# Dilated queries grouped by residue inside tiles of 128, and attention biases read as tables

## The chip, the cores and the metric

The kernel runs on one core of a Trainium2 chip. The metric is the device time of one execution in microseconds (us). The engines are TensorE (PE in the profile; its weight loads are listed apart as PEld), VectorE (DVE), ScalarE (ACT), GpSimd (POOL) and SyncE (SP), which issues most of the transfers (DMAs).

## The reference

One encoder layer and a final norm on 1024 tokens of width 1024, in float32.

```python
h = x
hn = rms_norm(h, norm_mix_g)
proj = hn @ w_in                              # q, k, v of 8 dilated and of 8 neighbourhood heads of 64
y_dil = dilated_mixture_attention(...)        # patterns (window, step): (128, 1), (512, 4), (2048, 16)
y_na  = neighbourhood_attention(..., rpb)     # 8 x 16 windows on a 16 x 64 grid, learned bias
h = h + concat(rms_norm(y_dil, g_out_dil), rms_norm(y_na, g_out_na)) @ w_out
h = h + hierarchical_moe(rms_norm(h, norm_ffn_g), ...)   # 1 of 4 groups, 2 of its 4 experts, width 256
y = rms_norm(h, norm_final_g)
```

The change lies in the dilated attention. A query at token t attends to the tokens t + j*d within half a window, for d = 1, 4 and 16; every score gets `- slope[head] * |distance|` with slope `0.5 ** (head + 1)`, and the three patterns are merged by their softmax denominators. Within the patterns of d = 4 and d = 16 a query meets only keys of its own residue modulo 4.

## The kernel before, in words

The kernel has three stages: norm, transposes and values (0 to about 120 us), attention (to about 530 us), and the router with 16 experts (to the end). Matrix products are in fp32r with each operand split in a high and a low part.

The attention stage works on eight pairs of heads, four dilated (`Dil`), then four of the neighbourhood kind (`Nbr`). Each pair has 16 steps, 8 for either head (`h` is 0 or 1, `n` is 0 to 7). The loop over steps (`for s in range(len(steps) + 4)`, L853) writes the order of all instructions by hand: step s issues the scores of its own step (`first`, with its matmuls on L411), the transposes of the probabilities of step s-2 (`second`, L509), and the product with the values of step s-3 (`third`, L534 and L545). Between these, `take` puts matmuls of the next pair's projection (L378), so that TensorE has work while the other engines do the softmax: `soft` on DVE (L424), the exponential on ACT (L430), and the evacuation in two parts (ACT L103, DVE L104).

In a dilated head the steps n = 0 to 3 are the near ones (d = 1 over a tile of 128 queries) and n = 4 to 7 the far ones, one for each residue r = n - 4 modulo 4. In each step two blocks of 128 queries are multiplied, each with the high and with the low part of the keys: four matmuls. The query block is the stationary operand (the weight load), the 256 keys are the moving one. Queries lie in `q_s` in the order of tokens, so a near block is 128 neighbouring columns and a far block is every fourth column:

```python
493                        qs = slice(512 * z + r, 512 * z + r + 509, 4)
```

Keys are already stored by residue. `fold` adds the two halves of a product and writes it to `ot`; in the far steps with r odd (L550) it writes two residues with a step of four columns. After the last step of a pair, `merge`, `merge2` and `store` weigh the near and the far result and store it to `y_dil` in DRAM (L558 to L601); these come in steps n = 1 to 3 of the next pair, which also hold the last projection matmuls of its queries and their evacuation (L401, L402). I call these steps the boundary of two pairs.

The bias of a dilated head is made on POOL in `prepare` (L462): a table of distances is halved in place for each head (L465) and the mask is added (L466). In a neighbourhood head POOL adds a mask that is loaded once to the learned bias (L623).

SP issues its DMAs strictly in the written order; a DMA that waits holds up all that are written behind it. Among them are the values (`va` L470 to L472, `vb` L477), the copy of keys into the other half of the partitions (`k_hh` L407), the projection weights (`w_raw` L152) and the stores.

Of the kernel before, what the change touches and what calls it, by code (L numbers as in the profile page):

```python
# [9 lines left out]
F32 = mybir.dt.float32  # L10
# [20 lines left out]
def shape_constants():  # L31

    p = np.arange(128)
    i, r = p // 4, p % 4
# [10 lines left out]
    mask = -8 * np.concatenate([m_a, m_b], 1).astype(np.float32)  # L45

# [12 lines left out]
    perm = np.zeros((128, 136), np.float32)  # L59
    perm[p, 4 * (p % 32) + 3] = 1.0  # L60
    perm[p, 132 + p // 32] = 1.0
# [7 lines left out]
    return {"dist": dist, "mask": mask, "na_mask": na_mask, "ident": np.eye(128, dtype=np.float32),  # L69
# [3 lines left out]
def build(nc, tc, a, ctx, dbg=None):  # L73
# [71 lines left out]
    with ExitStack() as att:  # L145
# [15 lines left out]
        factors = qk.tile([128, 2], F32, name="factors", bufs=1)  # L161
        perm = qk.tile([128, 136], F32, name="perm", bufs=1)
# [10 lines left out]
        with ExitStack() as ph:  # L173
# [125 lines left out]
            nc.vector.memset(factors[:, 0:1], 0.5)  # L299
            nc.vector.memset(factors[:, 1:2], 8.0)  # L300
# [37 lines left out]
        class Pair:  # L338
# [18 lines left out]
            def ps_view(self, ps, keys):  # L357
                if self.dil:
                    return ps.rearrange("p (i r) -> p r i", r=4) if keys else ps
                return ps.rearrange("p (r j c) -> p r j c", j=8, c=8)  # L360
# [48 lines left out]
            def scores(self, ps, h, qs, keys):  # L409
                for n, k in enumerate((self.kh, self.kl)):  # L410
                    nc.tensor.matmul(ps, self.q[h][:, qs], keys(k[h]), start=n == 0, stop=n == 1)  # L411
# [39 lines left out]
        class Dil(Pair):  # L451
# [22 lines left out]
            def late_loads(self, h):  # L474
                head = 2 * self.n + h
                vb = self.vb[h] = ap.tile([128, 8, 128], F32R, name="vb", tag="vb", bufs=1)
                nc.sync.dma_start(f(vb), vb_d[:, head * 128:(head + 1) * 128].rearrange("(k p) x -> p k x", p=128))  # L477

            def first(self, h, n):
# [4 lines left out]
                for z in range(2):  # L484
# [31 lines left out]
            def third(self, h, n, pt):  # L516
# [32 lines left out]
                if r % 2:  # L549
                    fold(self.ot[1][hs].rearrange("p (i r) -> p r i", r=4)[:, r - 1:r + 1], self.op,  # L550
                         lambda t: t.rearrange("p (r i) -> p r i", r=2))

            def merge(self):
# [3 lines left out]
                for h in range(2):  # L557
# [3 lines left out]
                                            perm[:, 132:136, None].to_broadcast([128, 4, 16]), op=ALU.mult)  # L561
                self.parts = parts

            def merge2(self):
                st, parts = self.stats, self.parts
                pb = bank("pt")
                for r in range(4):
                    nc.tensor.matmul(pb[:, 0:32], perm[:, 3 - r:131 - r], parts[:, :, :, 2 * r:2 * r + 2],
                                     start=r == 0, stop=r == 3)
                sb = ap.tile([128, 2, 2, 8], F32, name="sb")  # L570
                nc.vector.tensor_copy(sb.rearrange("p h z (q k) -> p k (h z) q", k=4),
                                      pb[:, 0:32].rearrange("p (k x q) -> p k x q", k=4, q=2))
                e = ap.tile([128, 2, 2, 8], F32, name="e")
                nm = ap.tile([128, 2, 8], F32, name="nm2")
# [4 lines left out]
                l2 = ap.tile([128, 2, 2, 8], F32, name="l2")  # L579
# [24 lines left out]
        class Nbr(Pair):  # L604


            def early_loads(self, h):
                if h == 0:
                    if self.n == 0:
                        Nbr.mask = ap.tile([128, 896], F32, name="na_mask", tag="mask", bufs=1)  # L610
                        nc.sync.dma_start(Nbr.mask, a["na_mask"])
                    self.nb = ap.tile([128, 2, 384], F32, name="nb", tag="dist", bufs=1)
                    nc.sync.dma_start(self.nb, nb_d[:, 2 * self.n:2 * self.n + 2, :])

            def prepare(self, h):
                head = 2 * self.n + h
                if h == 0:
                    nc.gpsimd.tensor_tensor(self.nb, self.nb, factors[:, 1:2, None].to_broadcast([128, 2, 384]),
                                            op=ALU.mult)
                bias = self.bias[h] = ap.tile([128, 896], F32, name="bias", tag="bias")  # L620
                nbv = self.nb[:, h].rearrange("p (r h c) -> p h r c", h=3, c=8)
                for c0, c1, h0, h1 in ((384, 640, 1, 3), (0, 384, 0, 3), (640, 896, 0, 2)):
                    nc.gpsimd.tensor_tensor(bias[:, c0:c1].rearrange("p (h r c) -> p h r c", r=16, c=8),  # L623
                                            Nbr.mask[:, c0:c1].rearrange("p (h r c) -> p h r c", r=16, c=8),
# [8 lines left out]
            def first(self, h, j):  # L633
# [6 lines left out]
                self.scores(sp[:, :n], h, slice(j * 128, j * 128 + 128), lambda k: k[:, c0 * 128:c1 * 128])  # L640
# [38 lines left out]
            def merge(self):  # L679
                self.rl = ap.tile([128, 8, 2], F32, name="rl")  # L680
# [172 lines left out]
        for s in range(len(steps) + 4):  # L853
# [14 lines left out]
            run_exps()  # L868
            run_slow(2)
# [925 lines left out]
```

## Time and profile before

| | us |
|---|---|
| median of 3 runs | 889.92 |
| lowest and highest run | 888.94, 892.41 |
| the profiled execution | 892.44 |
| its span in the trace | 890.7 |
| PE busy in the span | 832.3 (93%) |
| DVE, ACT, POOL busy | 558.5 (63%), 510.0 (57%), 220.9 (25%) |
| mean granted TensorE clock | 0.976 |

The span is the time from the first to the last instruction in the trace; the 1.7 us between it and the execution's time lie around it. A row of a timeline gives start, duration, engine, line, operation, output<-inputs, shape, count, and in brackets how long the engine had been idle and what ended that. Matmuls overlap, so the distance between two starts tells what one costs, and the duration does not. A `windows` row gives the busy time of each engine in a stretch, the granted clock, the mean busy share of the 16 DMA engines and the GB/s that they moved.

### The profile page before, as it was taken

The page shows a single profiled execution, that of the slowest core. Times are in us where ns is not written, and L with a number is a line of the kernel's source. Part 1 is how long each engine was busy: PE and PEld are TensorE (multiplying, and loading weights), DVE is VectorE, ACT ScalarE, POOL GpSimd, SP SyncE. Part 2 cuts the span into 40 slices and gives each one's busy share as a digit, 9 for nine tenths or more (in the row PEclk, how much of TensorE's full clock was granted, in tenths as well). Part 3 has the DMA queues.
Part 4 walks back from the last instruction along what each step waited for, and adds up shares of the span by engine and source line. Part 5 has one row for each costly group of instructions (what it writes and reads, how often), then busy time and mean ns, then how long its engine had stood idle before and what let it go on. Part 6 is the DMA issues. An engine that isn't in the chain of part 4 may idle for free. (4 is left out here: it accounts for less than half of the span.)

```text
span 890.7 us, 13312 instructions
## 1 busy us (share of the span) xinstructions
PE 832.3 (93%) x4492; PEld 693.2 (78%) x4492; DVE 558.5 (63%) x1249; ACT 510.0 (57%) x1079; POOL 220.9 (25%) x180
## 2 busy tenths in 40 slices
PE   8999999989999999999898999999799999999880
PEld 5888878979889888878787887887577787777760
DVE  4551125776767767666677753677786566959573
ACT  5441127757667576677575633543585566858570
POOL 4001122221232302332411100000442344635403
PEclk8999999999999999999999999998999999999995
DMA  6855452314343141534346747995798987999663
GB/s 238 286 210 165 126 159 65 105 48 108 96 136 105 54 137 48 148 100 120 76 160 195 265 144 239 357 343 216 233 354 250 317 220 209 357 324 304 181 257 121
DMA packets 129919, 168.72 MB, mean 189 GB/s; under 512 B 14875, under 2 KB 101403, under 8 KB 129824
## 3 DMA queue, kind: packets, MB, share of 16 engines
q1 hardware_dynamic: 119904, 143.58, 49.8%
q0 software_dynamic: 9936, 24.16, 9.8%
q8 instruction: 41, 0.67, 0.3%
q14 instruction: 38, 0.31, 0.1%
HBM read 129.93 MB, written 47.47 MB: 199 GB/s over the span
## 5 line engine op out<-in xcount | busy, mean ns | idle before, releaser
L103 ACT ACTIVATE pt_hi<-ps_pt 128x512 fp32r<-128x512 f32 (+2 forms) x128 | 67.6, 528 | 70.8 <-PE ps_pt L509 41.7
L378 PE MATMUL ps_mm<-xhi,w_lo 128*128 128x512 f32 x256 | 105.1, 411 | 1.1 <-POOL w_lo L104 1.1
L378 PE MATMUL ps_mm<-xlo,w_hi 128*128 128x512 f32 x256 | 105.0, 410 | 0.0
L378 PE MATMUL ps_mm<-xhi,w_hi 128*128 128x512 f32 x256 | 102.9, 402 | 0.0
L104 DVE TENSOR_TENSOR pt_lo<-ps_pt,pt_hi 128x512 fp32r<-128x512 f32 (+2 forms) x128 | 77.2, 603 | 31.8 <-ACT pt_hi L103 31.1
L104 POOL TENSOR_TENSOR w_lo<-w_raw,w_hi 128x1024 fp32r<-128x1024 f32 x16 | 38.3, 2392 | 229.5 <-ACT w_hi L103 229.5
L424 DVE CUSTOM_DVE_ANT_0 p<-ps_s,bias 128x256 f32<-128x256 f32 (+1 forms) x192 | 81.8, 450 | 18.2 <-PE ps_s L411 10.8
L104 DVE TENSOR_TENSOR g_lo<-raw_up,g_hi 128x1024 fp32r<-128x1024 f32 x64 | 75.5, 1220 | 25.2 <-ACT g_hi L103 25.1
L1419 PE MATMUL ps_mm<-g_hi,x_hi 128*128 128x512 f32 x184 | 76.0, 413 | 0.5 <-ACT x_hi L103 0.5
L1419 PE MATMUL ps_mm<-g_hi,x_lo 128*128 128x512 f32 x184 | 74.2, 403 | 2.2 <-DVE x_lo L104 2.2
L1419 PE MATMUL ps_mm<-g_lo,x_hi 128*128 128x512 f32 x184 | 73.9, 402 | 0.0
L430 ACT ACTIVATE p<-p,stats 128x256 f32<-128x256 f32 x128 | 63.7, 500 | 9.6 <-DVE stats L424 9.1
L103 ACT ACTIVATE g_hi<-raw_up 128x1024 fp32r<-128x1024 f32 x64 | 64.4, 1067 | 1.8 <-DMA raw_up<-in_w_up 0.8
L411 PE MATMUL ps_s<-k_hh,q_s 128*128 128x256 f32 (+1 forms) x192 | 60.7, 324 | 4.0 <-DMA k_hh<-k_hh 1.4
L411 PE MATMUL ps_s<-k_low,q_s 128*128 128x256 f32 (+1 forms) x192 | 62.6, 334 | 0.0
L411 PEld LDWEIGHTS ps_s<-k_hh,q_s 128*128 128x128 f32 x192 | 44.6, 232 | 10.9 <-DVE q_s L402 2.6
L378 PEld LDWEIGHTS ps_mm<-xhi,w_lo 128*128 128x128 f32 x256 | 48.7, 190 | 5.2 <-POOL w_lo L104 1.4
L1357 POOL DMA_INDIRECT xg<-hn_d,gi x30 | 41.3, 1377 | 40.1 <-PEq L1533 9.3
L378 PEld LDWEIGHTS ps_mm<-xhi,w_hi 128*128 128x128 f32 x256 | 48.7, 190 | 3.2
L378 PEld LDWEIGHTS ps_mm<-xlo,w_hi 128*128 128x128 f32 x256 | 48.4, 189 | 3.5
L411 PEld LDWEIGHTS ps_s<-k_low,q_s 128*128 128x128 f32 x192 | 44.6, 232 | 3.5
L430 ACT ACTIVATE p<-p,nm 128x384 f32<-128x384 f32 (+1 forms) x64 | 37.5, 586 | 15.2 <-DVE nm L424 14.8
(301 smaller groups left out, 2125.6 us busy)
## 6 DMA issues: line engine op xcount, KB each, us to landing
raw_up<-in_w_gate SPq DMA_DIRECT2D x32, 512.0 KB
raw_up<-in_w_up SPq DMA_DIRECT2D x32, 512.0 KB
raw_down<-in_w_down SPq DMA_DIRECT2D x16, 1024.0 KB
w_raw<-in_w_in SPq DMA_DIRECT2D x16, 512.0 KB
xt<-in_x SPq DMA_DIRECT2D x8, 512.0 KB
k_hh<-in_w_in SPq DMA_DIRECT2D x8, 512.0 KB
va_d<-vt SPq DMA_DIRECT2D x16, 256.0 KB
vb_d<-vt SPq DMA_DIRECT2D x8, 512.0 KB
```

Of the source, the lines that this page charges most:

```text
L103: nc.scalar.activation(hi, src, AF.Copy)
L104: (nc.gpsimd if pool else nc.vector).tensor_tensor(lo, src, f(hi), op=ALU.subtract)
L378: nc.tensor.matmul(ps, l[:, k, :], x[half][:, k, :], start=i == 0, stop=i == 23)
L411: nc.tensor.matmul(ps, self.q[h][:, qs], keys(k[h]), start=n == 0, stop=n == 1)
L424: nc.vector.tensor_tensor_reduce(out=p, in0=ps, in1=bias, scale=-0.125, scalar=3.0e38, op0=ALU.add, op1=ALU.min, accum_out=nm)
L430: nc.scalar.activation(p, p, AF.Exp, bias=nm, scale=-1.0, accum_out=l)
L1357: return nc.gpsimd.indirect_dma_start(out=x, out_offset=None, in_=src[:, :], in_offset=bass.IndirectOffsetOnAxis(ap=idx, axis=0), bounds_c ...
L1419: nc.tensor.matmul(ps, l[:, k, :], wt[:, k, :], start=i == 0, stop=i == 23)
```

## The change

1. The queries of a dilated pair are evacuated into `q_s` by residue inside each tile of 128: column 32r + i of a tile holds token 4i + r. The tables of distances and the merge's permutation follow that order; `ot` and `y_dil` hold it too, and `yd_load` puts tokens back in order when it reads `y_dil`.
2. A new step `regroup` copies a head's queries from `q_s` to a single buffer `qr`, where all 256 queries of a residue lie together. Four DMAs a head do so (eight half ones for the first head of a pair), each of 128-byte pieces. Far steps read `qr`.
3. The biases of the eight dilated heads come as finished tables from DRAM, one load a head. L465 and L466 go.
4. In a neighbourhood head the mask is loaded into the bias's buffer, once a head, and POOL adds the learned bias in place. Some small tiles of the merge have one buffer in place of two.

```diff
     p = np.arange(128)
-    i, r = p // 4, p % 4
+    i, r = p % 32, p // 32
...
+    bias = np.stack([np.float32(0.5 ** (h + 1)) * dist + mask for h in range(8)])
...
             def q_view(self, t, half):
                 if self.dil:
-                    return t[:, 512 * half:512 * half + 512]
+                    return t.rearrange("p (t r i) -> p t r i", r=4, i=32)[:, 4 * half:4 * half + 4]
...
             def early_loads(self, h):
-                if self.n == 0 and h == 0:
-                    Dil.dist = ap.tile([128, 768], F32, name="dist", tag="dist", bufs=1)
-                    Dil.mask = ap.tile([128, 896], F32, name="mask", tag="mask", bufs=1)[:, :768]
-                    nc.sync.dma_start(Dil.dist, a["dist"])
-                    nc.sync.dma_start(Dil.mask, a["mask"])
+                bias = self.bias[h] = ap.tile([128, 896], F32, name="bias", tag="bias")
+                nc.sync.dma_start(bias[:, :768], a["bias"][2 * self.n + h])
...
-                bias = self.bias[h] = ap.tile([128, 896], F32, name="bias", tag="bias")
-                nc.gpsimd.tensor_tensor(Dil.dist, Dil.dist, factors[:, 0:1].to_broadcast([128, 768]), op=ALU.mult)
-                nc.gpsimd.tensor_tensor(bias[:, :768], Dil.dist, Dil.mask, op=ALU.add)
...
+            def regroup(self, h, t0, t1):
+
+                if t0 == 0:
+                    self.qr = ap.tile([128, 1024], F32R, name="qr", bufs=1)
+                for r in range(4):
+                    nc.sync.dma_start(f(self.qr).rearrange("p (r t i) -> p r t i", r=4, i=32)[:, r, t0:t1],
+                                      f(self.q[h]).rearrange("p (t r i) -> p r t i", r=4, i=32)[:, r, t0:t1])
...
-                        qs = slice(512 * z + r, 512 * z + r + 509, 4)
+                        qs = slice(256 * r + 128 * z, 256 * r + 128 * z + 128)
...
-                    self.scores(sp[:, 256 * z:256 * z + 256], h, qs, keys)
+                    self.scores(sp[:, 256 * z:256 * z + 256], h, qs, keys,
+                                self.q[h] if n < 4 else self.qr)
...
-                    fold(self.ot[1][hs].rearrange("p (i r) -> p r i", r=4)[:, r - 1:r + 1], self.op,
-                         lambda t: t.rearrange("p (r i) -> p r i", r=2))
+                    fold(self.ot[1][hs].rearrange("p (t r i) -> p r t i", t=8, r=4)[:, r - 1:r + 1], self.op,
+                         lambda t: t.rearrange("p (r t i) -> p r t i", r=2, t=8))
...
+                self.bias[h] = ap.tile([128, 896], F32, name="bias", tag="bias")
+                nc.sync.dma_start(self.bias[h], a["na_mask"])
...
-            nc.sync.dma_start(yd[T], y_dil[128 * T:128 * T + 128, :])
+            nc.sync.dma_start(yd[T], y_dil[128 * T:128 * T + 128, :].rearrange("(r i) c -> i r c", r=4))
...
             run_exps()
+            if s < 64 and n == 0:
+                p.regroup(h, 0, 8 if h else 4)
+            if s < 64 and n == 1 and h == 0:
+                p.regroup(h, 4, 8)
             run_slow(2)
```

On SP the copies stand between the loads of the values. This is the second dilated pair, before, from the first head's `vb` to the second head's `k_hh` copy:

```order
L477 DMA vb<-vb_d 128x8x128
L601 DMA y_dil<-y_1701 128x4x128
L601 DMA y_dil<-y_1719 128x4x128
L152 DMA w_raw<-in_w_in 128x8x128
L329 DMA rp_d<-in_rpb 8x15x24 x8
L470 DMA va<-va_d 128x7x128
L472 DMA va<-va_d 128x2x128
L477 DMA vb<-vb_d 128x8x128
L407 DMA k_hh<-k_hh 64x1024 x2
```

And now the same place, where `qr` is the regrouped copy of the queries:

```order
L480 DMA qr<-q_s 128x4x32 x8
L459 DMA bias<-in_bias 128x768
L473 DMA vb<-vb_d 128x8x128
L606 DMA y_dil<-y_1718 128x4x128
L606 DMA y_dil<-y_1736 128x4x128
L154 DMA w_raw<-in_w_in 128x8x128
L330 DMA rp_d<-in_rpb 8x15x24 x8
L466 DMA va<-va_d 128x7x128
L480 DMA qr<-q_s 128x8x32 x4
L459 DMA bias<-in_bias 128x768
L473 DMA vb<-vb_d 128x8x128
L409 DMA k_hh<-k_hh 64x1024 x2
```

Eight half copies and a bias load come ahead of the first head's `vb`, four whole copies and a bias load between the second head's `va` and `vb`; the other DMAs keep their order.

On PE the first far step of the first pair stood so, with the scores read from `q_s`:

```order
L378 MATMUL ps_mm<-xhi_82,w_lo 128x512
L411 MATMUL ps_s<-k_hh,q_s 128x256
L411 MATMUL ps_s<-k_low_91,q_s 128x256
L378 MATMUL ps_mm<-xhi_83,w_hi 128x512
L378 MATMUL ps_mm<-xlo_85,w_hi 128x512
```

Now it reads `qr`:

```order
L380 MATMUL ps_mm<-xhi_82,w_lo 128x512
L413 MATMUL ps_s<-k_hh,qr 128x256
L413 MATMUL ps_s<-k_low_91,qr 128x256
L380 MATMUL ps_mm<-xhi_83,w_hi 128x512
L380 MATMUL ps_mm<-xlo_85,w_hi 128x512
```

Nothing moves on PE: every matmul keeps its place, and 128 of the 384 of the scores have another weight operand and may wait for a DMA. On PE 61 of these 384 matmuls waited for something before (7 of them for two things), and 92 do now (21 for two). ACT's order is unchanged, DVE loses one memset, and POOL loses the 16 instructions of L465 and L466.

## Rows read from the trace of the kernel before

**Rows 1.** Windows: the dilated stretch, the rest of attention, and the experts. Columns: stretch, its length, busy time and instruction count of PE, PEld, DVE, ACT and POOL, granted clock, DMA share, GB/s.

```profile
120.00:345.00 225.00, 217.51 (x1324) 191.59 (x1323) 150.77 (x432) 149.55 (x394) 58.14 (x35) 1.00 0.36 98
345.00:530.00 185.00, 176.83 (x997) 150.21 (x997) 127.83 (x308) 116.60 (x277) 39.40 (x37) 1.00 0.46 138
530.00:890.00 360.00, 322.21 (x1664) 259.80 (x1662) 235.92 (x438) 202.61 (x337) 108.04 (x96) 0.95 0.82 269
```

**Rows 2.** Timeline of PE: the four score matmuls of a far step (n = 7, first pair) and the matmul behind them, then of a near step (n = 0) likewise.

```profile
150.42 0.28 PE L411 MATMUL ps_s<-k_hh,q_s 128*128 128x256 f32 x1
150.54 0.40 PE L411 MATMUL ps_s<-k_low,q_s 128*128 128x256 f32 x1
150.77 0.40 PE L411 MATMUL ps_s<-k_hh,q_s 128*128 128x256 f32 x1
151.00 0.40 PE L411 MATMUL ps_s<-k_low,q_s 128*128 128x256 f32 x1
151.24 0.40 PE L378 MATMUL ps_mm<-xhi,w_hi 128*128 128x512 f32 x1
...
153.55 0.28 PE L411 MATMUL ps_s<-k_hh,q_s 128*128 128x256 f32 x1
153.66 0.28 PE L411 MATMUL ps_s<-k_low,q_s 128*128 128x256 f32 x1
153.78 0.28 PE L411 MATMUL ps_s<-k_hh,q_s 128*128 128x256 f32 x1
153.91 0.28 PE L411 MATMUL ps_s<-k_low,q_s 128*128 128x256 f32 x1
154.02 0.39 PE L378 MATMUL ps_mm<-xhi,w_hi 128*128 128x512 f32 x1
```

**Rows 3.** Timeline of PEld: a weight load of the same far step and one of the same near step; then the view of line L411 (shortest, median and longest weight load in ns, and the sequencer's waits).

```profile
150.87 0.33 PEld L411 LDWEIGHTS ps_s<-k_low,q_s 128*128 128x128 f32 x1
...
153.55 0.19 PEld L411 LDWEIGHTS ps_s<-k_low,q_s 128*128 128x128 f32 x1
```

```profile
L411 PEld LDWEIGHTS ps_s<-k_low,q_s x192: 187/188/334, 130.4 to 517.3; 128*128 128x128 f32 x192
L411 PEldq EVENT_SEMAPHORE  x7: 51/51/51, 126.2 to 473.7; - x7
```

**Rows 4.** One head's steps in the second pair (h = 1): windows from its first score matmul to the next pair's.

```profile
208.50:232.70 24.20, 24.20 (x152) 21.91 (x151) 16.86 (x49) 18.51 (x50) 5.65 (x3) 1.00 0.43 115
```

**Rows 5.** Timeline of DVE at the boundary of the first and the second pair: the two far folds there, a near fold a little before, and the query evacuation that follows; then the group of L442 (count, busy us and mean ns).

```profile
175.97 0.69 DVE L442 TENSOR_TENSOR ot<-ps_o,fold 64x512 f32<-64x512 f32 x1
...
181.64 1.07 DVE L442 TENSOR_TENSOR ot<-ps_o,fold 64x512 f32<-64x512 f32 x1 [0.91 <-ACT fold L438]
...
183.54 0.68 DVE L402 TENSOR_TENSOR q_s<-ps_mm,q_s 64x512 fp32r<-64x512 f32 x1
...
190.37 1.07 DVE L442 TENSOR_TENSOR ot<-ps_o,fold 64x512 f32<-64x512 f32 x1 [0.42 <-ACT fold L438]
```

```profile
L442 DVE TENSOR_TENSOR ot<-ps_o,fold 64x512 f32<-64x512 f32 x36 | 30.9, 858 | 21.1 <-ACT fold L438 20.6
```

**Rows 6.** Timeline of PE at the same boundary: every row with idle time before it, and the first far score behind.

```profile
184.28 0.39 PE L411 MATMUL ps_s<-k_hh,q_s 128*128 128x256 f32 x1 [0.54 <-DVE q_s L402]
...
186.10 1.05 PE L568 MATMUL ps_pt<-parts,perm 128*128 128x32 f32 x8 [0.62 <-DVE parts L558]
...
191.50 0.66 PE L594 MATMUL ps_o<-ident,ot 128*128 128x128 f32 x4 [0.20 <-DVE ot L442]
...
193.51 1.25 PE L594 MATMUL ps_o<-ident,ot 128*128 128x128 f32 x8 [0.88 <-DVE y L596]
194.52 0.48 PE L411 MATMUL ps_s<-k_hh,q_s 128*128 128x256 f32 x1
```

**Rows 7.** The groups of the evacuations of queries and keys on DVE (L402), and of POOL's bias work; then who waited longest for the bias.

```profile
L402 DVE TENSOR_TENSOR q_s<-ps_mm,q_s 64x512 fp32r<-64x512 f32 x32 | 22.0, 688 | 24.2 <-ACT q_s L401 24.1
L402 DVE TENSOR_TENSOR k_low<-ps_mm,k_hh 64x512 fp32r<-64x512 f32 x32 | 22.0, 688 | 29.8 <-ACT k_hh L401 29.8
L466 POOL TENSOR_TENSOR bias<-dist,mask 128x768 f32<-128x768 f32 x8 | 14.7, 1840 | 0.6
L465 POOL TENSOR_TENSOR dist<-dist,factors 128x768 f32<-128x768 f32 x8 | 11.7, 1465 | 17.8 <-DMA dist<-in_dist 17.8
```

```profile
DVE p L424 <- POOL bias L623: 1.4, 1, 1.4
```

**Rows 8.** Windows again, for the price of DMA pieces: a stretch in which one `w_raw` load runs (512 KB in 1024 pieces of 512 bytes), and one in which such a load runs beside 3072 pieces of 4, 16 and 64 bytes (`g_c`, `w_group`, `w_router`).

```profile
170.00:174.00 4.00, 4.00 (x27) 3.69 (x26) 3.24 (x12) 3.17 (x9) 3.07 (x2) 1.00 0.45 131
424.25:427.75 3.50, 3.10 (x21) 2.41 (x19) 3.40 (x9) 1.19 (x3) 3.05 (x4) 1.00 0.85 156
```

**Rows 9.** Timeline of SP: issues of a copy inside SBUF, of a store with 512-byte pieces, and of the load with 64-byte pieces.

```profile
161.79 1.87 SPq L407 DMA_DIRECT2D k_hh<-k_hh  x2
195.44 1.80 SPq L601 DMA_DIRECT2D y_dil<-y  x2
425.23 1.93 SPq L771 DMA_DIRECT2D wr<-in_w_router  x1
```

**Rows 10.** Timeline of PE at the last pair's begin, where a DMA was late.

```profile
473.82 0.36 PE L411 MATMUL ps_s<-k_hh,q_s 128*128 128x256 f32 x1 [1.39 <-DMA k_hh<-k_hh]
```

More of the change, by code (lines that the diff above doesn't have):

```diff
@@ L57, in shape_constants @@
     na_mask = -8 * np.concatenate(parts, 1).astype(np.float32)
-    perm = np.zeros((128, 136), np.float32)
-    perm[p, 4 * (p % 32) + 3] = 1.0
-    perm[p, 132 + p // 32] = 1.0
+    perm = np.zeros((128, 228), np.float32)
+    perm[p, 96 + p % 32] = 1.0
+    perm[p, 224 + p // 32] = 1.0
     tri = (p[:, None] < p[None, :]).astype(np.float32)
@@ L68, in shape_constants @@
     small[:, 56] = 1024 + p
-    return {"dist": dist, "mask": mask, "na_mask": na_mask, "ident": np.eye(128, dtype=np.float32),
+    return {"bias": bias, "na_mask": na_mask, "ident": np.eye(128, dtype=np.float32),
             "tri": tri, "iota": iota, "small": small, "perm": perm, "zeros": np.zeros((128, 372), np.float32)}
@@ L159, in split_w @@
             return hi, lo
[L161 to L162 removed]
+        factors = qk.tile([128, 1], F32, name="factors", bufs=1)
+        perm = qk.tile([128, 228], F32, name="perm", bufs=1)
         k_low = [[qk.tile([128, 1024], F32R, name="k_low%d%d" % (n, h), bufs=1) for h in range(2)] for n in range(2)]
@@ L358, in ps_view @@
                 if self.dil:
-                    return ps.rearrange("p (i r) -> p r i", r=4) if keys else ps
+                    return ps.rearrange(*(("p (i r) -> p r i",) if keys else ("p (t i r) -> p t r i",)), **(
+                        dict(r=4) if keys else dict(r=4, i=32)))
                 return ps.rearrange("p (r j c) -> p r j c", j=8, c=8)
@@ L407, in double, with scores @@
                     nc.sync.dma_start(f(self.kh[h])[own[1 - h], :], f(self.kh[h])[own[h], :])
-            def scores(self, ps, h, qs, keys):
+            def scores(self, ps, h, qs, keys, q):
                 for n, k in enumerate((self.kh, self.kl)):
-                    nc.tensor.matmul(ps, self.q[h][:, qs], keys(k[h]), start=n == 0, stop=n == 1)
+                    nc.tensor.matmul(ps, q[:, qs], keys(k[h]), start=n == 0, stop=n == 1)
         slow = []
@@ L567, in merge2 @@
                 for r in range(4):
-                    nc.tensor.matmul(pb[:, 0:32], perm[:, 3 - r:131 - r], parts[:, :, :, 2 * r:2 * r + 2],
+                    nc.tensor.matmul(pb[:, 0:32], perm[:, 96 - 32 * r:224 - 32 * r], parts[:, :, :, 2 * r:2 * r + 2],
                                      start=r == 0, stop=r == 3)
-                sb = ap.tile([128, 2, 2, 8], F32, name="sb")
+                sb = ap.tile([128, 2, 2, 8], F32, name="sb", bufs=1)
                 nc.vector.tensor_copy(sb.rearrange("p h z (q k) -> p k (h z) q", k=4),
                                       pb[:, 0:32].rearrange("p (k x q) -> p k x q", k=4, q=2))
-                e = ap.tile([128, 2, 2, 8], F32, name="e")
-                nm = ap.tile([128, 2, 8], F32, name="nm2")
+                e = ap.tile([128, 2, 2, 8], F32, name="e", bufs=1)
+                nm = ap.tile([128, 2, 8], F32, name="nm2", bufs=1)
                 nc.vector.tensor_tensor(nm, st[:, :, 0, :], sb[:, :, 0, :], op=ALU.min)
@@ L608, in early_loads @@
                 if h == 0:
[L609 to L612, printed above, removed]
+                    self.nb = ap.tile([128, 2, 384], F32, name="nb", bufs=1)
                     nc.sync.dma_start(self.nb, nb_d[:, 2 * self.n:2 * self.n + 2, :])
+                self.bias[h] = ap.tile([128, 896], F32, name="bias", tag="bias")
+                nc.sync.dma_start(self.bias[h], a["na_mask"])
             def prepare(self, h):
@@ L617, in prepare @@
                 if h == 0:
-                    nc.gpsimd.tensor_tensor(self.nb, self.nb, factors[:, 1:2, None].to_broadcast([128, 2, 384]),
+                    nc.gpsimd.tensor_tensor(self.nb, self.nb, factors[:, :, None].to_broadcast([128, 2, 384]),
                                             op=ALU.mult)
-                bias = self.bias[h] = ap.tile([128, 896], F32, name="bias", tag="bias")
+                bias = self.bias[h]
                 nbv = self.nb[:, h].rearrange("p (r h c) -> p h r c", h=3, c=8)
@@ L623, in prepare @@
                     nc.gpsimd.tensor_tensor(bias[:, c0:c1].rearrange("p (h r c) -> p h r c", r=16, c=8),
-                                            Nbr.mask[:, c0:c1].rearrange("p (h r c) -> p h r c", r=16, c=8),
+                                            bias[:, c0:c1].rearrange("p (h r c) -> p h r c", r=16, c=8),
                                             nbv[:, h0:h1], op=ALU.add)
@@ L639, in first @@
                 sp = bank("s")
-                self.scores(sp[:, :n], h, slice(j * 128, j * 128 + 128), lambda k: k[:, c0 * 128:c1 * 128])
+                self.scores(sp[:, :n], h, slice(j * 128, j * 128 + 128), lambda k: k[:, c0 * 128:c1 * 128], self.q[h])
                 nm = ap.tile([128, 1], F32, name="nm", bufs=4)
```

9 lines of the change are left out of this document (4 added, 5 removed).

## The prediction

> **What bounds the kernel now.** I read the windows first. In the dilated stretch TensorE is busy for 217.5 of 225 us at full granted clock, DVE and ACT for 151 and 150 us, and the DMA engines for a share of 0.36 [rows 1]. So TensorE sets the time there, and a microsecond taken off its queue shortens the stretch unless something else comes up. The rest of attention is nearly as full, and the change gives it no shorter instruction [rows 1]. Everything behind is issued in one fixed order after the attention, so I let a gain made before 345 us reach the end in full.
>
> Next I read PE's timeline start by start. In a far step the first score matmul starts at 150.42 and the matmul behind the four starts at 151.24: 0.82 us. In a near step it is 153.55 to 154.02: 0.47 us [rows 2]. Both have four matmuls of 256 columns. The weight loads tell why: 0.33 us in the far step, where the queries are every fourth column, 0.19 us in the near one, where they are neighbours; the line's loads run from 187 to 334 ns [rows 3]. The matmuls of a far step follow each other at 0.23 us, the pace of the slow loads, and not at 0.12 us [rows 2].
>
> **The change part by part.**
>
> *Far scores from `qr`.* A far step's weights become 128 neighbouring columns, and its keys are one run as before. I price it as a near step: 0.82 - 0.47 = 0.35 us saved. There are 4 pairs x 2 heads x 4 steps = 32 far steps: 32 x 0.35 = 11.2 us. Is TensorE the limit in them? In one whole head it is busy for all 24.2 of 24.2 us, with DVE at 16.9 and ACT at 18.5 [rows 4]. With 4 x 0.35 = 1.4 us less, ACT would be at 18.5 of 22.8, or 81%, so I keep the whole gain.
>
> [...]
>
> *Far folds.* A far fold writes `ot` with a step of four and takes 1.07 us; a near one takes 0.69 [rows 5]. The group's 30.9 us fit that: 16 x 1.07 + 20 x 0.69 = 30.9. Now the fold writes runs of 32 columns, and I price it as a near one: 0.38 us less. Inside a pair PE does not wait for DVE, so that hides. At the boundary of two pairs it does: PE idles 0.54 + 0.62 + 0.20 + 0.88 = 2.24 us, and DVE works through its queue [rows 6]. The first fold (181.64) stands ahead of the query evacuation (183.54) that PE waits for, so that wait falls by 0.38. The second (190.37) ends the 0.20 and stands ahead of the 0.88; another 0.38. That is 0.76 us a boundary, and with three boundaries between dilated pairs 2.3 us. Bounds: nothing, if ACT is late there instead, and all idle of three boundaries, 6.7 us.
>
> *More waits on PE.* Far scores wait for DMAs that should have landed, so only the second wait of an instruction costs: 21 - 7 = 14 of them by the order of the two kernels, at 0.051 us each [rows 3], make 0.7 us. Nothing, if the queue hides them; I take 0.7.
>
> *The copies.* A head has 4096 pieces of 128 bytes (128 partitions x 8 tiles x 4 residues), 512 KB. No row shows such pieces inside SBUF. One 512 KB load with 512-byte pieces takes 4.00 x 0.45 = 1.80 us of all engines, 28 ns a piece on one of 16. The stretch with 3072 tiny pieces beside such a load takes 3.50 x 0.85 = 2.98; the rest, 1.18 us, is 6 ns a piece [rows 8]. Between these a head's copies take 1.5 to 7.2 us of 24.2. Near the tiny pieces in size, I take some 10 ns, 2.6 us. They are off the path as long as they land in time. For the first head of a pair the late half of the queries is ready at 183.54 + 0.68 = 184.2 [rows 5], and the first far score comes at 194.5 [rows 6]: 10.3 us for four issues and the transfer. An issue on SP takes 0.9 to 1.9 us in the slow rows [rows 9], so four take 3.7 to 7.7; only the first of the four is needed at 194.5, the others each a step later. For the second head the single buffer is free after the last far score of the first head, one step ahead of its own first, and it has four steps. Behind the copies on SP stand the bias and `vb`; `vb` waits for the previous head's last product anyway, which comes in step 2 or later of this head. Price: nothing.
>
> *Evacuation of queries.* It now reads PSUM with a step of four, as that of keys already does: 688 ns for either on DVE [rows 7]. Nothing.
>
> *Biases.* POOL loses 14.7 + 11.7 = 26.4 us [rows 7] that no engine waited for; the one wait for a bias, 1.4 us, is on L623 [rows 7], which stays. Nothing. The tables' loads are 384 KB a head, 0.75 of the 1.80 us above, 1.35 us of DMA time, and land a head before use.
>
> *Masks in the neighbourhood heads.* Eight loads of 448 KB, 1.6 us of DMA each by the same row, on the same queue, in place of one. They are issued five steps ahead of POOL. At the last pair the queue is tight: PE waits 1.39 us there for the keys' copy [rows 10]. Bounds 0 to 2 x 1.6 = 3.2 us; I take 0, since the mask is written well ahead of that copy.
>
> *The sum.* -11.2 - 2.3 + 0.7 = -12.8 us. The profiled execution of 892.44 would become 879.6. It lies 2.5 us over the median of the runs; from the median, 889.92 - 12.8 = 877.1 us. The terms' bounds for this case: -11.2 - 6.7 = -17.9, or 872.0, and -11.2 + 0.7 + 3.2 = -7.3, or 882.6.
>
> **The rivals.**
>
> *The chain through ACT and DVE takes over.* The far steps become shorter but softmax does not, and transposes two steps later wait for it. For it: ACT at 81% with waits between engines, and boundaries at which DVE has already no slack [rows 6]. Against it: a head in which PE never idles [rows 4]. If half of the 11.2 us is lost so and the folds give nothing: 889.92 - 5.6 + 0.7 = 885.0.
>
> *The stride is not the price.* The far loads would be slow for another reason, and stay slow. Then only folds and waits are left: 889.92 - 2.3 + 0.7 = 888.3. For it: far and near steps differ in their keys too. Against it: the load itself is long, and it reads only queries [rows 3]. [...]
>
> *Slower: the copies clog the DMA queue.* The place is the first far score of each head, which then waits for `qr`, with `vb` behind it. Other traffic in a head takes 0.43 x 24.2 = 10.4 us [rows 4] and the bias 1.35, so 12.4 of 24.2 us are left, 48 ns for each of 4096 pieces on 16 engines. Above that the head is slower than before. At 60 ns: 15.4 + 11.8 = 27.2, 3.0 us more in each of eight heads, +24, or 914 us. For it: no row shows small pieces from SBUF to SBUF. Against it: it takes more than a 512-byte piece's 28 ns [rows 8].
>
> [...]
>
> *A wait on SP* for queries or for the free buffer holds up a weight load behind it, and gives back about the gain: 889.
>
> **How the numbers follow.** Chances: the forecast 0.70, the chain 0.16, the stride 0.04, SP 0.04, clogging 0.06. The predicted time is 877.1. Its own range is 872 to 882.6; the range for 8 in 10 takes in the chain's 885.0 and ends there, and below I add half a microsecond for the spread of medians: 871.5 to 885. A measurement here can tell about 0.5% or 4.5 us: the forecast is faster by 1.4%, the chain's 885.0 by 0.55%, of which I count three quarters as faster. Faster 0.70 + 0.12 = 0.82; within 0.5% the chain's other 0.04, the stride's 0.04 and SP's 0.04, 0.12; slower 0.06.
>
> **What would show it.** Far steps right: the longest weight load of the score line near 0.21 us and 0.47 us from first score to the next matmul; wrong: 0.33 stays. Folds right: a group mean near 0.69 us, and a boundary's idle near 1.5 us. Copies right: no wait of PE for `qr`; wrong: PE idle ahead of the first far step with a DMA as releaser, or `vb` late. The sum is wrong if PE's idle time between 120 and 345 grows by more than a few microseconds, or if the neighbourhood stretch, 185 us now, grows.

## The result and the profile after

The changed kernel takes 878.31 us (median of 4 runs, 877.14 to 880.08) against 889.43 us before in the same series, a ratio of 0.9871 with a 95% interval of 0.9842 to 0.9900. In a later series it took 878.90 us against 891.12, ratio 0.9855 (0.9840 to 0.9869). The forecast was 877.1 us in a range of 871.5 to 885.0. The gain comes from the stretch that the prediction named, but a cost that it did not have stands ahead of that stretch.

The page of the changed kernel, engine totals and packets (the profiled execution took 877.14 us, its span is 875.3):

```profile
PE 818.0 (93%) x4492; PEld 677.7 (77%) x4492; DVE 551.9 (63%) x1248; ACT 511.0 (58%) x1079; POOL 191.3 (22%) x164
...
DMA packets 165329, 178.55 MB, mean 204 GB/s; under 512 B 48619, under 2 KB 135147, under 8 KB 165232
```

PE has the same 4492 matmuls and is busy for less time (832.3 us before).

The dilated steps alone, as windows from the first score of the first dilated pair to the last far score. First the kernel before, over its stretch:

```profile
130.39:342.00 211.61, 204.29 (x1261) 180.79 (x1259) 145.88 (x423) 144.31 (x384) 53.34 (x32) 1.00 0.33 92
```

then the changed kernel over its own, and the head of [rows 4], which here begins at 206.36:

```profile
133.11:331.24 198.13, 192.34 (x1260) 168.62 (x1259) 139.38 (x423) 144.69 (x384) 30.58 (x18) 1.00 0.55 133
206.36:229.26 22.90, 22.90 (x153) 20.48 (x151) 15.78 (x47) 18.10 (x49) 2.39 (x1) 1.00 0.73 175
```

The stretch is 13.5 us shorter: 12.0 us of it are busy time of PE (204.29 to 192.34), 1.5 us are idle time (7.32 to 5.79). The head of [rows 4] takes 22.9 us in place of 24.2, and PE is still never idle in it, with ACT busy for 18.1 us. The stretch also begins 2.7 us later, at 133.11 in place of 130.39.

The spans of the two executions differ by more than these two, by 15.4 us. The neighbourhood's steps are not the reason: from the last far score to the last score it takes 175.4 us in both. Behind the last score it is 373.2 us before and 368.6 after, but there single executions differ: in the seven profiles of this case in which the last score was read, one of each run, this part takes between 368.6 and 374.3 us. So the 4.6 us are not put down to the change.

PE's timeline of the far step of [rows 2], and the view of the score line that answers to [rows 3]:

```profile
152.11 0.28 PE L413 MATMUL ps_s<-k_hh,qr 128*128 128x256 f32 x1
152.22 0.29 PE L413 MATMUL ps_s<-k_low,qr 128*128 128x256 f32 x1
152.35 0.28 PE L413 MATMUL ps_s<-k_hh,qr 128*128 128x256 f32 x1
152.47 0.29 PE L413 MATMUL ps_s<-k_low,qr 128*128 128x256 f32 x1
152.60 0.39 PE L380 MATMUL ps_mm<-xhi,w_hi 128*128 128x512 f32 x1
```

```profile
L413 PEld LDWEIGHTS ps_s<-k_low,qr x64: 187/188/192, 142.4 to 331.1; 128*128 128x128 f32 x64
...
L413 PEldq EVENT_SEMAPHORE  x21: 51/51/51, 128.9 to 463.6; - x21
```

The step takes 152.60 - 152.11 = 0.49 us, against 0.82 before and 0.47 in a near step. No load of a far query takes longer than 192 ns. The 21 second waits are there as the order had shown, each of 51 ns.

The folds, as DVE's group and as the two at the first boundary of pairs, and PE's idle rows at that boundary, for [rows 5] and [rows 6]:

```profile
L444 DVE TENSOR_TENSOR ot<-ps_o,fold 64x512 f32<-64x512 f32 x36 | 24.6, 684 | 20.8 <-ACT fold L440 20.4
```

```profile
181.68 0.68 DVE L444 TENSOR_TENSOR ot<-ps_o,fold 64x512 f32<-64x512 f32 x1 [0.91 <-ACT fold L440]
...
190.04 0.68 DVE L444 TENSOR_TENSOR ot<-ps_o,fold 64x512 f32<-64x512 f32 x1 [0.43 <-ACT fold L440]
```

```profile
183.93 0.39 PE L413 MATMUL ps_s<-k_hh,q_s 128*128 128x256 f32 x1 [0.18 <-DVE q_s L404]
...
185.76 1.05 PE L573 MATMUL ps_pt<-parts,perm 128*128 128x32 f32 x8 [0.62 <-DVE parts L563]
...
192.78 1.25 PE L599 MATMUL ps_o<-ident,ot 128*128 128x128 f32 x8 [0.88 <-DVE y L601]
...
193.79 0.36 PE L413 MATMUL ps_s<-k_hh,qr 128*128 128x256 f32 x1
```

PE's idle time here was 0.54 + 0.62 + 0.20 + 0.88 = 2.24 us and is 0.18 + 0.62 + 0.88 = 1.68. The first far score of the pair follows without idle time, so the regrouped queries had landed. One wait shrank, that which a far fold stood ahead of, and the 0.20 that a far fold ended is gone; the 0.88 stayed. The prediction counted three such boundaries. There is a fourth, from the last dilated pair to the first neighbourhood pair, where the kernel before has this row:

```profile
356.94 1.25 PE L594 MATMUL ps_o<-ident,ot 128*128 128x128 f32 x8 [0.52 <-DVE y L596]
```

In the changed kernel PE has no idle time at that place.

What is new ahead of the stretch is seen in PE's timeline of the value projection, in which the tokens (`xhi`, `xlo`) are the stationary operand and the weight matrix of the values (`wv_hi`, `wv_lo`) is the moving one, 512 columns at a time. The same moment in both kernels, and for each the 100th and the last of the 384 matmuls of this projection. Before:

```profile
40.47 0.40 PE L222 MATMUL ps_o<-wv_hi,xhi 128*128 128x512 f32 x1
...
78.07 0.39 PE L222 MATMUL ps_o<-wv_hi,xhi 128*128 128x512 f32 x1
78.30 0.39 PE L222 MATMUL ps_o<-wv_lo,xhi 128*128 128x512 f32 x1
78.52 0.39 PE L222 MATMUL ps_o<-wv_hi,xlo 128*128 128x512 f32 x1
78.75 0.39 PE L222 MATMUL ps_o<-wv_hi,xhi 128*128 128x512 f32 x1
...
107.76 0.40 PE L222 MATMUL ps_mm<-wv_hi,xlo 128*128 128x512 f32 x1
```

After:

```profile
41.53 0.39 PE L224 MATMUL ps_o<-wv_hi,xhi 128*128 128x512 f32 x1
...
78.43 0.40 PE L224 MATMUL ps_o<-wv_hi,xhi 128*128 128x512 f32 x1
78.67 0.39 PE L224 MATMUL ps_o<-wv_lo,xhi 128*128 128x512 f32 x1
78.89 0.40 PE L224 MATMUL ps_o<-wv_hi,xlo 128*128 128x512 f32 x1
79.13 0.39 PE L224 MATMUL ps_o<-wv_hi,xhi 128*128 128x512 f32 x1
...
110.40 0.39 PE L224 MATMUL ps_mm<-wv_hi,xlo 128*128 128x512 f32 x1
```

Three matmuls took 0.68 us and take 0.70. The line, its operands' shapes and its order are the same. From the 100th to the last it was 67.29 us and is 68.87: 1.6 us of the delay. Nearly all of the other 1.1 us arose before the 100th, and how much of that is the same effect can't be told, since executions differ ahead of the first score by up to 1.5 us: of two runs below that have these matrices at one place, one has it at 129.58 us and one at 131.07. The change does not touch these matmuls. What it does touch is where their moving operand lies: `perm` grew from 136 to 228 columns, and all tiles that are placed behind it, in its own pool and in the two that lie on top of it, `wv_hi` and `wv_lo` among them, moved by 384 bytes in each partition, while `xhi` and `xlo` stayed where they were.

### The profile page after: what moved, and what is told of

The parts are those of the page before. It is cut to its first block, busy times and chain, and to the rows that moved or that the text cites. A ratio compares the mean times of both kernels' runs of the same rounds, so it can differ in the third digit from the quotient of the medians.

```text
span 875.3 us, 13434 instructions
## 1 busy us (share of the span) xinstructions
PE 818.0 (93%) x4492; PEld 677.7 (77%) x4492; DVE 551.9 (63%) x1248; ACT 511.0 (58%) x1079; POOL 191.3 (22%) x164
## 5 line engine op out<-in xcount | busy, mean ns | idle before, releaser
L1368 POOL DMA_INDIRECT xg<-hn_d,gi x30 | 38.8, 1294 | 37.0 <-PEq L1544 9.1
L756 PE MATMUL ps_mm<-whi,w_hi 128*128 128x512 f32 x128 | 44.5, 405 | 0.3 <-DVE k_hh L759 0.3
L1430 PEld LDWEIGHTS ps_mm<-g_hi,x_lo 128*128 128x128 f32 x184 | 34.5, 188 | 11.4 <-DVE x_lo L106 3.1
L106 DVE TENSOR_TENSOR d_lo<-raw_down,d_hi 128x1024 fp32r<-128x1024 f32 x31 | 36.6, 1221 | 7.8 <-ACT d_hi L105 7.6
L413 PE MATMUL ps_s<-k_hh,q_s 128*128 128x256 f32 (+1 forms) x128 | 38.3, 311 | 3.3 <-DMA k_hh<-k_hh 1.3
```

Of the source, the lines that this page charges most:

```text
L106: (nc.gpsimd if pool else nc.vector).tensor_tensor(lo, src, f(hi), op=ALU.subtract)
L413: nc.tensor.matmul(ps, q[:, qs], keys(k[h]), start=n == 0, stop=n == 1)
L756: nc.tensor.matmul(ps, y[:, l, k, :], w[0][:, k, cc], start=i == 0, stop=i == 11)
L1368: return nc.gpsimd.indirect_dma_start(out=x, out_offset=None, in_=src[:, :], in_offset=bass.IndirectOffsetOnAxis(ap=idx, axis=0), bounds_c ...
L1430: nc.tensor.matmul(ps, l[:, k, :], wt[:, k, :], start=i == 0, stop=i == 23)
```

## The experiments

Three questions were open. Does each term of the sum come from the edit it was put down to? Are the copies free, or only just hidden? And what costs the time ahead of the stretch? Runs of one series share the runs of the kernel before (medians 890.2, 891.1 and 890.6 us in the three series), so ratios are compared, not medians.

**The far scores alone.** The kernel before, with only the columns of a far query block changed:

```diff
-                        qs = slice(512 * z + r, 512 * z + r + 509, 4)
+                        qs = slice(256 * r + 128 * z, 256 * r + 128 * z + 128)
```

> The kernel before, in which the far steps read 128 neighbouring query columns in place of every fourth; the queries then do not belong to the residue of the keys, so the far pattern's result is left out in effect. No copies, no other fold, no tables. Theory 1 (the slow weight load of strided columns sets the far step): 0.35 us in each of 32 far steps, 11.2 us less than before, about 878; the longest load of the score line falls from 0.33 to 0.21 us or less, and a far step's four scores take 0.47 us. Rival 2 (the load is hidden, and the gain of the change came from the folds on DVE and from POOL): within 2 us of before.

Measured: 878.45 us (876.28 to 882.14), ratio 0.9878 (0.9856 to 0.9901), which is 10.9 us of 889.9. The dilated steps, first score to last far score, went from 211.6 to 200.9 us. The view of the score line has no slow load left:

```profile
L411 PEld LDWEIGHTS ps_s<-k_low,q_s x192: 187/188/193, 130.5 to 506.5; 128*128 128x128 f32 x192
```

The stride of the weight operand is the price, and not the far step's keys, which are the same here as before. This run and the next two compute another far result, so the router may choose other experts; behind the last score their profiles show 370.4, 370.6 and 374.3 us, so the last one may have lost 1 us or so there.

**The far folds alone.** The kernel before, with the far products written side by side, so in other columns of `ot`:

```diff
-                    fold(self.ot[1][hs].rearrange("p (i r) -> p r i", r=4)[:, r - 1:r + 1], self.op,
+                    fold(self.ot[1][hs].rearrange("p (r i) -> p r i", r=4)[:, r - 1:r + 1], self.op,
```

> The kernel before, in which only the far folds write neighbouring columns of ot in place of every fourth, so that the order of the far result is left wrong. Theory 1: a far fold falls from 1.07 to 0.69 us, PE's idle time at each of three boundaries falls by 0.76 us, the time by 2.3 us (bounds 0 to 3). Rival 2 (the folds carry the gain): 8 us or more. Rival 3 (DVE waits for ACT there instead): 0, with PE's idle time as before.

Measured: 886.73 us (885.78 to 889.08), ratio 0.9968 (0.9957 to 0.9979): 2.9 us. The dilated steps took 209.3 us, 2.3 less than before, which is the predicted term; the 0.52 us at the fourth boundary went besides. In the run with the far scores alone that wait is still there, 0.49 us, so it is the fold's. PE's idle rows at the first boundary are those of the changed kernel, within 0.03 us:

```profile
183.82 0.39 PE L411 MATMUL ps_s<-k_hh,q_s 128*128 128x256 f32 x1 [0.15 <-DVE q_s L402]
...
185.64 1.05 PE L568 MATMUL ps_pt<-parts,perm 128*128 128x32 f32 x8 [0.61 <-DVE parts L558]
...
192.66 1.25 PE L594 MATMUL ps_o<-ident,ot 128*128 128x128 f32 x8 [0.89 <-DVE y L596]
```

**The change without the far scores' gain.** The changed kernel, whose far steps read `qr` with a step of four again (so other queries than they should):

```diff
-                        qs = slice(256 * r + 128 * z, 256 * r + 128 * z + 128)
+                        qs = slice(512 * z + r, 512 * z + r + 509, 4)
```

> The changed kernel, in which the far steps read every fourth column of the copy qr; the queries are then mixed over the residues, which leaves the far pattern's result out in effect. Copies, tables, masks and folds are all there. Theory 1: 11.2 us more than the changed kernel, about 889.5, so 0 to 2 us less than before, with loads of 0.33 us. Rival 2: as fast as the changed kernel, 878. Rival 3 (the copies and the further loads cost something that the gain hides): slower than before by that.

Measured: 890.90 us (887.53 to 894.22), ratio 1.0006 (0.9990 to 1.0023). Its view of the score line:

```profile
L413 PEld LDWEIGHTS ps_s<-k_low,qr x64: 307/329/334, 141.2 to 341.2; 128*128 128x128 f32 x64
```

The loads are slow again, and the gain of the folds, which is still in it, has gone as well: something else in the change costs about 3 us. Its first score stands at 131.9 us, 1.5 later than in the kernel before; its dilated steps take 209.4 us, as in the run with the folds alone.

**A move of the tiles alone.** The kernel before, with `perm` widened by 96 columns that nobody uses:

```diff
-        perm = qk.tile([128, 136], F32, name="perm", bufs=1)
+        perm = qk.tile([128, 232], F32, name="perm", bufs=1)[:, :136]
```

> The kernel before with the tile perm made 384 bytes a partition wider (its columns unused), which moves all tiles of the first two stages up by as much as the change does, and nothing else. In the profile after, the first score came 2.7 us later than before, with matmuls of the value projection 0.234 us apart in place of 0.227. Theory D (the place of the tiles in SBUF sets that): the first score at 133.1 us and the median 2.7 us above before. Rival E (a difference between executions or chips): the first score anywhere from 130 to 133, and the median within 1.5 us of before.

Measured: 893.09 us (889.51 to 895.78), ratio 1.0035 (1.0020 to 1.0049): 3.1 us slower (1.8 to 4.4). Nothing is computed, loaded or ordered in another way. The windows from 60 to 104 us, in the value projection, count the matmuls that ran in them, those under way at 60 us among them. First the kernel before, then this one:

```profile
60.00:104.00 44.00, 44.00 (x196) 36.41 (x195) 11.37 (x16) 11.08 (x15) 4.77 (x2) 1.00 0.50 150
```

```profile
60.00:104.00 44.00, 44.00 (x191) 35.38 (x190) 10.95 (x15) 10.67 (x14) 4.80 (x2) 1.00 0.46 142
```

With PE busy throughout and the clock at 1.00, 196 matmuls ran in the same 44 us in which 191 run now; the changed kernel's row counts 192, four of them transposes of 128 columns. The first score came at 132.0 us, 1.6 later than before and not the 2.7 expected. The dilated steps took 211.7 us, as before. So the cost that the trace shows lies ahead of them; 1.6 us is less than the 3.1 of the medians, and where the rest lies is not shown.

**A move by 128 bytes.** As above, with 168 columns.

> The kernel before with perm 168 columns wide instead of 136, of which 136 are used: all that follows lies 128 bytes further on in each partition; nothing else differs. Theory (the pace of the value projection hangs on the place of its tiles, and any move away from the old place costs it): spacing 0.234 us in the value projection and about 893 us, as with 384 bytes. Rival (only some places cost): 0.227 us, and the time of the kernel before, 889.9. Either is possible; the run is to say which.

Measured: 894.11 us (890.91 to 896.59), ratio 1.0029 (1.0014 to 1.0043), which is 2.6 us (1.2 to 3.8), and its row of the 44 us counts 192, with four such transposes among them. A third of the move costs as much, within the noise.

**The changed kernel with the table out of the way.** `perm` lies in the attention's pool, and `factors` is widened so that the tiles behind it lie 512 bytes ahead of their place in the kernel before:

```diff
-        factors = qk.tile([128, 1], F32, name="factors", bufs=1)
-        perm = qk.tile([128, 228], F32, name="perm", bufs=1)
+        factors = qk.tile([128, 16], F32, name="factors", bufs=1)[:, 0:1]
...
-            nc.sync.dma_start(perm, a["perm"])
...
+        perm = ap.tile([128, 228], F32, name="perm", bufs=1)
...
+        nc.sync.dma_start(perm, a["perm"])
```

> The changed kernel, except that the 228-column table perm lies in the attention's memory and is loaded there, so that the tiles that follow it are no longer 384 bytes further on in each partition than in the kernel before (they lie 512 bytes ahead of their old place). Theory (the place of the tiles costs the value projection its pace): the matmuls of the value projection stand 0.227 us apart again, the first far score comes back from 133.1 to about 130.3 us, and the time is 875.4 us, 2.9 below the changed kernel. Rival (the 3 us come from what else the change puts ahead of the first score: the table's load, the masks, the issues): the spacing stays at 0.234 and the time at 878.3.

Beside it, on the same chip, ran the changed kernel once more:

> The changed kernel once more, beside the others on the same chip: 878.3 us, spacing in the value projection 0.234 us, first far score at about 133 us.

Measured: 875.24 us (875.13 to 876.58), ratio 0.9823 (0.9811 to 0.9836), against 878.90 us and 0.9855 (0.9840 to 0.9869) for the changed kernel. The intervals do not touch. The window of the value projection is back at 196:

```profile
60.00:104.00 44.00, 44.00 (x196) 36.40 (x195) 10.95 (x14) 11.74 (x16) 4.76 (x2) 1.00 0.48 143
```

The first score came at 131.07 us and not at the 130.3 expected; the repeated changed kernel had it at 132.06 and not at 133, so this moment differs by about 1 us between executions, and the count in the window is the better witness. This version beats both kernels.

**The same without the change.** The kernel before with `perm` moved in the same way:

> The kernel before with perm in the attention's memory, loaded there, as in the run perm_moved: the tiles behind it move 512 bytes ahead, and nothing of the change is in it. Theory (a move by 512 bytes leaves the value projection its pace of 0.227 us, a move by 128 or 384 does not): the time of the kernel before, 889.9, so that perm_moved gave back what the move by 384 bytes had cost and no more. Rival (the later load of perm is worth something by itself): about 887 us.

Measured: 890.43 us (888.44 to 892.74), ratio 0.9997 (0.9982 to 1.0012), and 195 matmuls in the 44 us. The later load of the table and a move by 512 bytes together change nothing that can be told (between 1.6 us faster and 1.1 slower), where the rival had some 3 us faster.

All runs together give thirteen profiles, and for twelve of them the row of these 44 us was read. In the six with the weight matrix in its old place or 512 bytes ahead of it, it counts 195 or 196 matmuls; in the six with it 128 or 384 bytes further on, 190 to 192. From the first to the last of the final 216 matmuls of the value projection it is 48.88 us in the old place and 48.86 at 512 bytes ahead, 0.227 us apart in the mean, and 50.25 us at 128 bytes further on and 50.24 at 384, 0.234 us apart.

**Biases and masks alone.** The changed kernel's tables, mask loads and single small buffers in the kernel before; far queries stay at a step of four, and `perm` keeps its width:

```diff
+                bias = self.bias[h] = ap.tile([128, 896], F32, name="bias", tag="bias")
+                nc.sync.dma_start(bias[:, :768], a["bias"][2 * self.n + h])
...
-                nc.gpsimd.tensor_tensor(Dil.dist, Dil.dist, factors[:, 0:1].to_broadcast([128, 768]), op=ALU.mult)
-                nc.gpsimd.tensor_tensor(bias[:, :768], Dil.dist, Dil.mask, op=ALU.add)
...
+                self.bias[h] = ap.tile([128, 896], F32, name="bias", tag="bias")
+                nc.sync.dma_start(self.bias[h], a["na_mask"])
```

> The kernel before with the second half of the change alone: the biases of the dilated heads loaded as tables, the neighbourhood's mask loaded into the bias's place; the far queries stay at stride four, without a regroup, and perm keeps its width, so that the tiles behind it stay where they were. Theory (POOL's work on the biases lay beside PE's, and nobody waited for it): no change, 889.9 us. Rival (the loads into the bias's place come late for POOL, the upper bound of the masks' term): 3.2 us slower, 893.1, with a wait of POOL for in_na_mask.

Measured: 891.60 us (888.59 to 895.42), ratio 1.0010 (0.9996 to 1.0024), so between 0.4 us faster and 2.1 slower: no change that can be told, and less than the rival's 3.2. The wait that the rival named exists once, for 1.0 us:

```profile
POOL bias L627 <- DMA bias<-in_na_mask: 1.0, 1, 1.0
```

The 26.4 us of POOL work that went bought nothing, as nobody had waited for it.

**The copies twice, back to back.** The changed kernel with each transfer of `regroup` issued twice:

```diff
-                for r in range(4):
+                for r in (0, 0, 1, 1, 2, 2, 3, 3):
```

> The changed kernel with each of the regroup's transfers issued twice, so 96 instead of 48 of them, into the same places. Theory (they run beside PE work and nobody waits for them): no change, 878.3 us, and no idle time of PE put down to qr. [...]

Measured: 921.68 us (920.98 to 925.75), ratio 1.0347 (1.0328 to 1.0366). My theory had said 878.3, and by the number alone the queues would be clogged. The rows say something else. This is SP's timeline over one head's copies, four issues in the changed kernel, then eight in this one:

```profile
153.44 3.61 SPq L480 DMA_DIRECT2D qr<-q_s  x4
```

```profile
159.08 16.95 SPq L480 DMA_DIRECT2D qr<-q_s  x8
```

and this is the longest wait of PE that came of it:

```profile
270.74 0.58 PE L413 MATMUL ps_s<-k_hh,qr 128*128 128x256 f32 x1 [7.25 <-DMA qr<-q_s]
```

A repeat writes the same bytes as the transfer before it, and the program makes it wait on SP, by a semaphore, until that one has landed, four times in each set. So it was the time SP stands that grew, to more than four times, and with it that of everything written behind it. PE waits 20.6 us for `qr` and 11.1 us for `vb` in all, and the clock is granted at a mean of 0.91 between 240 and 300 us, where it is 1.00 in the changed kernel. The edit had tested a chain of waits of its own making.

**The copies twice, set after set.** The same transfers, bytes and places, with the repeats behind a whole set:

```diff
-                for r in range(4):
+                for r in (0, 1, 2, 3, 0, 1, 2, 3):
```

> The changed kernel with each of the regroup's transfers issued twice again, but a whole set of four and then the set again, where the run copies_twice issued each transfer and its repeat back to back; bytes, packets and places are the same as there. Theory (copies_twice lost its time because SP held each repeat until the transfer before it, which writes the same place, had landed: 8 issues took 16.95 us in one row there, against 3.77 us for 4 in the changed kernel): SP now stands once per regroup and not four times, the group of 8 takes about 8 us, and most of the 43 us go: 878 to 890 us. Rival (the doubled packets themselves are too many for the queues): the packets are as many as in copies_twice, and the time stays near 921 us.

Measured: 878.93 us (878.19 to 881.20), ratio 0.9876 (0.9854 to 0.9898): the time of the changed kernel. SP at the same place:

```profile
152.51 8.40 SPq L480 DMA_DIRECT2D qr<-q_s  x8
```

The packets are 198,867 in all, as in the run before (198,866), and no engine waits for `qr`. The transfers have room for twice their number. One more set is some 33,500 packets, about 4,200 a head. From 133 to 330 us the DMA share of this run and of the changed kernel differ by 0.14:

```profile
133.00:330.00 197.00, 191.19 (x1252) 167.46 (x1251) 139.27 (x422) 143.95 (x382) 30.57 (x18) 1.00 0.70 154
```

```profile
133.00:330.00 197.00, 191.21 (x1251) 167.45 (x1250) 138.79 (x422) 144.09 (x382) 30.20 (x18) 1.00 0.56 134
```

That is 0.14 x 197 = 27.6 us of all engines for one more set of some eight heads, 3.4 us a head, or about 13 ns for each of 256 pieces on an engine.

## Why the prediction was right, and what it lacked

*Far scores, -11.2 us.* Right in mechanism and nearly in size. The load fell from 334 to 188 ns, the step to 0.49 us, and the edit alone gave 10.9 us (8.8 to 12.8) and a stretch shorter by 10.7. A far step gained 0.33 us and not 0.35. That the stride sets the time of the load, against the rival that it is not the price, two kernels show that differ in nothing else: neighbouring columns took 188 ns and every fourth column 307 to 334 ns.

*Far folds, -2.3 us.* Right, and for the reason given: 0.68 us for a fold in place of 1.07, a group mean of 684 ns, most of the idle time before the query scores went, and so did the 0.20. The run with this edit alone shortened the stretch by 2.3 us and the kernel by 2.9 (1.9 to 3.8). That the 2.3 was met is partly luck. At the first boundary 0.56 us of idle time went in the changed kernel and not 0.76, because the 0.88 ended with `y` on DVE and stayed; the rest of the 2.3 lies elsewhere in the stretch. And the fourth boundary, which the prediction did not count, gave another 0.5 us behind it.

*Extra waits of PE, +0.7 us.* They are there, 21 of 51 ns, but no time can be put down to them: the two edits alone shorten the stretch by 10.7 + 2.3 = 13.0 us, and the whole change by 13.5. The lower bound, nothing, was the better value.

*Copies, nothing.* Right, and the price of a piece, some 10 ns, was near the 13 measured. The rival in which they clog the queue needed more than 48 ns.

*Evacuation, biases, masks, nothing.* Right within what can be told: the evacuation takes 689 ns, 688 before, and the run with biases and masks alone gives 0.9 us more (0.4 less to 2.1 more). PE's wait for the keys' copy at the last pair, the place where the masks might have shown [rows 10], is 1.3 us after the change, and 1.7 in the repeat.

*The rivals.* ACT and DVE did not take over: PE has no idle time in the head of [rows 4] with ACT at 79%, and the idle time of the stretch fell. SP's queue held nobody up as the change has it. It does as soon as the transfers wait for one another, which the first of the doubled runs showed at 43 us.

*What the sum lacked.* It had a term only for instructions that the diff names. The gain in the dilated steps, 13.5 us in the trace, is close to the 12.8 forecast. But the larger `perm` moved the weight matrix of the value projection, and that had no term: it costs 1.6 us or more in the traces, 3.1 us (1.8 to 4.4) as an edit alone. The time came out 1.2 us above the forecast, and that this is so little is in part luck. With the move undone the change gains 15.8 us (14.6 to 16.8), 3.0 more than forecast, and the cost of the move took most of that back.

Not settled is a small rest. The terms measured alone, -10.9 - 2.9 + 0.9, sum to -12.9 us against these 15.8. The intervals of the single terms are wide enough to hold the difference. In part the edits help each other: PE's waits for the queries' evacuation sum to 1.3 us before, to 1.6 with the far scores alone, to 0.5 with the folds alone and to 0.6 in the changed kernel, so there the folds take off 1.0 us behind the far scores and 0.8 as an edit alone.

## What to carry to other kernels

In this kernel a weight operand read with a step of four was paid on TensorE itself, with 307 to 334 ns a load in place of 188 and 0.33 us a step. So where PE is the limit, look at the longest load of a line beside its median, and let a transfer put the columns side by side where the DMA engines have room for it (here a share of 0.33 before the change and 0.55 with it). When an edit changes the size of a tile, all tiles behind it in the pool move (here by 384 bytes, which alone cost 3.1 us); run the old kernel with that move alone before judging the edit. When doubling a transfer to see if it is free, keep the repeats from waiting for each other, or the run measures the wait (921.68 us back to back, 878.93 set after set).

## What the runs showed of the hardware that was not expected

- In these runs the pace of a matmul went with the place of tiles in SBUF. With the same instructions, busy PE and a granted clock of 1.00, matmuls of 512 columns stood 0.227 us apart in the mean with the moving operand in its old place or 512 bytes ahead of it, and 0.234 us with it 128 or 384 bytes further on. The median weight load takes 187 to 188 ns before and after. The slower pace is not peculiar to the move: behind the value projection, in the same trace of the kernel before, twelve matmuls of 512 columns (the projection of queries and keys, L378) take 2.80 us, which is 0.233 each as well; the rows are below. Why was not found. All tiles behind `perm` moved together, by these three amounts; that it is the moving operand is argued, since PE reads no other of them in these matmuls.
- Pieces of 128 bytes from SBUF to SBUF took about 13 ns each on one of 16 engines, by the estimate from the DMA shares above, and 8192 of them a head still delayed no one: 878.93 us, and no wait for `qr`.

The first matmul of that projection in the kernel before, and the one twelve further on:

```profile
108.00 0.39 PE L378 MATMUL ps_mm<-xhi,w_hi 128*128 128x512 f32 x1
...
110.80 0.39 PE L378 MATMUL ps_mm<-xhi,w_hi 128*128 128x512 f32 x1
```
